# Two value products over 512 columns at once, with their weights in units of two row groups

## The chip, the cores and the metric

One core of a Trainium2 chip. The metric is the time of one launch on the device in microseconds; lower is better. The engines of the core are named as the profile names them: PE (matrix products), PEld (its weight loads), DVE and ACT (vector and scalar work), POOL, and SP, which issues the transfers.

## The reference, cut to what matters

One encoder layer over 512 tokens of width 1024, in float32. Three token mixers run side by side, their results are gated and summed, and a layer of 16 experts follows.

```python
z = jnp.einsum('bsd,df->bsf', x, w_in[l])
q_na, k_na, v_na, q_g, k_g, v_g, q_m, gate_logits = jnp.split(z, _split_points(), axis=-1)
y_na  = neighbourhood_attention(q_na, k_na, v_na, rpb)      # 8 heads of 64
y_gqa = gqa_attention(q_g, k_g, v_g, ...)                   # 8 query heads of 64, 2 key/value heads
mkv = jnp.einsum('bmd,df->bmf', mem, w_mem_kv[l])           # 256 memory tokens
mk, mv = jnp.split(mkv, 2, axis=-1)
y_mem = memory_attention(q_m, mk, mv)                       # 4 heads of 128
merged = jnp.sum(gates * proj, axis=2)
x = layer_norm(DN_ALPHA * x + merged @ w_out)
x = layer_norm(DN_ALPHA * x + expert_choice_ffn(x))
```

The change concerns two of these products: `mv`, 256 memory tokens by 1024 by 512 columns, and `v_na`, 512 tokens by 1024 by 512 columns.

## The kernel before

**Products in three parts.** Float32 operands are split into a high part (a copy to the type float32r, on ACT) and a low part (the source less the high part, on DVE); `hi_lo` (L91) issues both. A product is three matmuls for each of the 8 groups of 128 rows of the contraction: high by high, high by low, low by high, all added up in one bank of PSUM.

**Weights as a stream.** The weights of the mixers lie in memory as 74 units of 128 x 1024 (512 KB), in the order of use. `Stream` (L137) takes them through three steps: `_dma` issues the load of a unit into a raw buffer (SP), `_split` makes its high and low part (ACT, DVE), `take` hands it to a product. `prefetch(n)` splits ahead until n units beyond those taken are split, and then issues loads until two units (`AHEAD_DMA`) beyond the split ones are on their way. A load needs a raw buffer: units 2 to 9 have one each, all others share two (`raw_twin`), so a load waits for the subtraction of the unit two before it. A split needs a home: there are three for high parts (two buffers `whi`, one in `los`) and three for low parts (in `los`), taken in turn (`hi_tile`, `lo_tile`), so a split waits for the last product of the unit three before it.

A narrow unit (`nu` on the host) holds 256 columns of 512 rows: two of them make a product over 256 columns, which `n_chunk` (L290) issues for one block of 128 tokens: 8 x 3 = 24 matmuls, 256 columns each. A unit of the last product of the mixers (`wide`, units 66 to 73) holds 512 columns of 256 rows.

**The memory mixer.** `g_mem` (L317) makes four key products (`k_item`), the values (`v_item`, L347: two halves of 256 columns, two token blocks each, with the last two parts of the split of x among them), and four query products (`q_item`). Its units are 0 to 3, 4 to 7 and 8 to 11.

**The order of the work around the second product.** The order of every engine's instructions is the order in which the program issues them; each engine works through its own list. `run` (L782) drives a generator of products and, at each of its yields, takes a step of the attention pipeline (`Attn.step`, L754) at a given rate. One step issues, for three units of attention in flight: the scores of the newest (S) on PE, the transposes of the one before (T), the value product of the one before that (PV); then the softmax of the newest (row maxima on DVE, two exponentials on ACT), the evacuation of the transposes (half on DVE, half on ACT), the normalisation (DVE) and the split of the result. The scores have two banks of PSUM, the transposes two, the plain products three.

`g_na_v` (L461) is the value product of the neighbourhood mixer, units 30 to 33: two halves of 256 columns, for each half four token blocks, with a yield after each block, which makes eight yields. The last steps of the grouped attention fall on the first of them. After it two transfers copy the values shifted by half a tile (`v_shift`, L474), the transfers of the position bias follow, and then the mixer's query and key products (nqk, units 34 and 35).

```python
    run(g_branch(2, True), 1.0, 3)
    run(g_na_v(), 1.0)
    at.drain()
    na_bias(0)
    run(g_na_qk(0))
```

The experts' weights come through a ring of buffers (`Ring`), loaded as buffers become free.

Of the kernel before, what the change touches and what calls it, by code (L numbers as in the profile page):

```python
# [10 lines left out]
F32R = mybir.dt.float32r  # L11
# [7 lines left out]
P = 128  # L19
D = 1024  # L20
S = 512
KD = 8
NT = 4
# [41 lines left out]
def layer_kernel(ctx: ExitStack, tc: tile.TileContext, xt, xn, first0, wu, bgate, rpb, gains, wrt,  # L65
# [14 lines left out]
    def R(tag, shape, name, dt=F32, bufs=None):  # L80
        return rp.tile(shape, dt, name=name, tag=tag, bufs=bufs)
# [46 lines left out]

    los = R("Q9", [P, 4, 1024], "los", F32R)

    def hi_tile(i):
        if i % 3 == 2:
            return los[:, 3]
        return R("hi", [P, 1024], f"whi{i}", F32R, bufs=2)


    class Stream:  # L137
# [23 lines left out]
        def _split(self):  # L161
            i = self.ns
            if i >= self.nd:
                self._dma()
            raw = self.raw.pop(i)
            if i == N_UNITS - 1:
                both = R("VS", [P, 2, 1024], "wlast", F32R)
                hi, lo = both[:, 0], both[:, 1]
            else:
                hi = hi_tile(i)  # L170
                lo = lo_tile(i)
            hi_lo(hi, lo, raw)
            self.hl[i] = (hi, lo)
            self.ns += 1
# [7 lines left out]
        def take(self, n=1):  # L182
# [2 lines left out]
            r = [self.hl.pop(self.used + j) for j in range(n)]  # L185
            self.used += n
            return r

    def lo_tile(i):
        return los[:, i % 3]  # L190

    after = {}
    ws = Stream()
# [96 lines left out]
    def n_chunk(acc, us, ah, al, m, hooks={}):  # L290
        c = slice(m * P, (m + 1) * P)
        for k in range(KD):
# [4 lines left out]
            nc.tensor.matmul(acc, ah[:, k, c], lo, start=False, stop=False)  # L297
            nc.tensor.matmul(acc, al[:, k, c], h, start=False, stop=(k == KD - 1))

    def spin(n):  # L300
        for _ in range(n):
            nc.tensor.matmul(warm[:, :P], ident, ident, start=True, stop=True)
# [14 lines left out]
    def g_mem():  # L317
        zz = R("Q3", [P, 4, 1024], "mkvzs")
        ST["A5"] = zz[:, 0:2]
        ST["A6"] = zz[:, 2:4]  # L320
        mk = ST["A5"][:, 0].rearrange("p (h t) -> p h t", h=4)
        mv = ST["A6"][:, 0].rearrange("p (m f) -> p m f", m=2)
        qm = R("Q2", [P, 4, S], "qmT")
        ST.update(mkT=mk, mv=mv, qmT=qm)

        def k_item(h):
            u, = ws.take()
            ws.prefetch()
            acc = PB("mm", f"mk{h}")
            if h == 0:  # L330
                first_unit(acc[:, :256])
            else:
                t_unit(acc[:, :256], u, memh, meml, h == 1)
            if h >= 2:
                split_x(h - 2)
            yield
            nc.vector.tensor_copy(mk[:, h], acc[:, :256])

        def q_item(h):
            u, = ws.take()  # L340
            ws.prefetch()
            acc = PB("mm", f"qm{h}")
            t_unit(acc, u, xh, xl)
            yield
            nc.scalar.activation(qm[:, h], acc, AF.Copy, scale=1.0 / math.sqrt(128.0))

        def v_item(q):  # L347
            us = ws.take(2)
            for m in range(2):
                acc = PB("mm", f"mv{q}{m}")  # L350
                n_chunk(acc[:, :256], us, memh, meml, m)
                ws.prefetch(1 + m)
                if q == 0:
                    split_x(2 + m)
                yield
                nc.scalar.copy(mv[:, m, q * 256:(q + 1) * 256], acc[:, :256])

        for h in range(4):
            yield from k_item(h)
        for q in range(2):  # L360
            yield from v_item(q)
        for h in range(4):
            yield from q_item(h)

# [96 lines left out]
    def g_na_v():  # L461
        v = ST["b01"][:, 0:2].rearrange("p a (b f) -> p (a b) f", f=S)
        ST["v_na"] = v
        for q in range(2):
            us = ws.take(2)
            for m in range(NT):
                acc = PB("mm", f"nv{q}{m}")
                n_chunk(acc[:, :256], us, xh, xl, m)
                ws.prefetch(2 if m == NT - 1 else 1)
                yield  # L470
                nc.scalar.copy(v[:, m, q * 256:(q + 1) * 256], acc[:, :256])
        vs = R("VS", [P, 3, S], "v_shift")
        ST["v_shift"] = vs
        nc.sync.dma_start(vs[0:64], v[64:128, 0:3])  # L474
        nc.sync.dma_start(vs[64:128], v[0:64, 1:4])
# [1210 lines left out]
def _prep(inp):  # L1686
    import numpy as np
    f = np.float32
    x = np.asarray(inp["x"])[0]
    xp = _perm(x)  # L1690
    w_in = np.asarray(inp["w_in"])[0]
    w_mem = np.asarray(inp["w_mem_kv"])[0]
    w_br = np.asarray(inp["w_branch"])[0]
    w_out = np.asarray(inp["w_out"])[0]

    def tu(w, c):
        return w[:, c:c + 128].reshape(8, 128, 128).swapaxes(0, 1).reshape(128, 1024)

    def nu(w, c, h):
        return w[h * 512:(h + 1) * 512, c:c + 256].reshape(4, 128, 256).swapaxes(0, 1).reshape(128, 1024)  # L1700

    def wide(w, c, kp):
        return w[kp * 256:(kp + 1) * 256, c:c + 512].reshape(2, 128, 512).swapaxes(0, 1).reshape(128, 1024)

    def pu(g, jp):
        return w_br[g][:, jp * 256:(jp + 1) * 256].reshape(4, 128, 256).swapaxes(0, 1).reshape(128, 1024)

    gate = lambda g, j: tu(w_in, 2816 + g * 1024 + j * 128)
    mk = lambda h: [tu(w_mem, h * 128)]
    mv = lambda q: [nu(w_mem, 512 + q * 256, h) for h in range(2)]  # L1710
    qm = lambda h: [tu(w_in, 2304 + h * 128)]
    units = mk(0) + mk(1) + mk(2) + mk(3) + mv(0) + mv(1) + qm(0) + qm(1) + qm(2) + qm(3)
    units += [nu(w_in, 1536 + q * 256, h) for q in (2, 0, 1) for h in range(2)]
    for jp in range(4):
        units += [gate(2, 2 * jp), gate(2, 2 * jp + 1), pu(2, jp)]
    units += [nu(w_in, 1024 + q * 256, h) for q in range(2) for h in range(2)]
    qk = lambda hp: [tu(w_in, hp * 128), tu(w_in, 512 + hp * 128)]
    units += qk(0)
    for jp in range(4):
        units += [gate(1, 2 * jp), gate(1, 2 * jp + 1), pu(1, jp)]  # L1720
        if jp < 3:
            units += qk(jp + 1)
    units += [gate(0, j) for j in range(8)]
    units += [pu(0, jp) for jp in range(4)]
    units += [wide(w_out, o * 512, kp) for o in range(2) for kp in range(4)]
    assert len(units) == N_UNITS

    t = np.arange(512)
    b, r, c = t // 64, (t // 8) % 8, t % 8
    orig = r * 64 + b * 8 + c  # L1730
    inv = (f(10000.0) ** (-np.arange(0, 32, 2, dtype=f) / f(32))).astype(f)
    ang = np.concatenate([r.astype(f)[:, None] * inv, (b * 8 + c).astype(f)[:, None] * inv], -1).astype(f)
    csn = np.stack([np.cos(ang), np.sin(ang)], 1).astype(f)
    csn = csn.reshape(4, 128, 2, 32).swapaxes(0, 1)
    p = np.arange(128)
    s = 8 * (p // 64) + p % 8
    nmask = np.zeros((128, 3, 32), f)
    for ty in range(3):
        v = -8 * ty + np.arange(32)[None, :]
        lo = s - 8  # L1740
        lo = np.maximum(lo, 0) if ty == 0 else (np.minimum(lo, 0) if ty == 2 else lo)
        ok = (v >= lo[:, None]) & (v < lo[:, None] + 16)
        nmask[:, ty] = np.where(ok, 0.0, NEG)
    before = (orig[:, None] <= orig[None, :]).astype(np.float16)
    tri = np.stack([before[:128, 128:256], before[128:256, :128], before[:128, :128]])
    rpbp = np.zeros((8, 15, 63), f)
    rpbp[:, :, 16:47] = np.asarray(inp["na_rpb"])[0]
    rpbr = np.stack([rpbp[:, 7 - rr:15 - rr] for rr in range(8)])
    memt = np.asarray(inp["mem"])[0].T.reshape(8, 128, 256).swapaxes(0, 1)
    return {  # L1750
        "xt": xp.T.reshape(8, 128, 512).swapaxes(0, 1),
        "xn": xp.reshape(4, 128, 1024).swapaxes(0, 1),
        "first0": np.concatenate([memt.reshape(128, 4, 512), units[0].reshape(128, 4, 256)], -1),
        "wu": np.stack(units),
        "bgate": np.asarray(inp["b_gate"])[0].reshape(24, 128).T,
        "rpb": rpbr,
        "gains": np.stack([np.asarray(inp["gqa_q_gain"])[0], np.asarray(inp["gqa_k_gain"])[0]]),
        "wrt": np.asarray(inp["w_router"])[0].reshape(8, 128, 16).swapaxes(0, 1),
        "lnp": _norm_rows(*(np.asarray(inp[n])[0] for n in ("ln1_g", "ln1_b", "ln2_g", "ln2_b"))),
        "lnt": np.stack([np.asarray(inp[n])[0].reshape(8, 128).T for n in ("ln1_g", "ln1_b")], 1),  # L1760
        "wx": _expert_rows(np.asarray(inp["w_gate_up"])[0], np.asarray(inp["w_down"])[0]),
        "csn": csn, "nmask": nmask, "tri": tri,
        "iota": np.broadcast_to(np.arange(1, 65, dtype=f), (128, 64)),
    }
# [23 lines left out]
```

## Time and profile before

| | |
|---|---|
| median of 3 runs | 968.36 us (968.03 to 968.84) |
| the profiled execution | 967.9 us |
| its span, first to last instruction | 966.1 us, granted clock 0.998 |
| PE busy | 943.5 us, 98% of the span |
| value product of the memory (mv) | 96 matmuls of 256 columns, 19.7 to 31.2 us |
| value product of the last mixer (nv) | 192 matmuls of 256 columns, 212.0 to 247.4 us, five attention steps among them |

In the tables of the profile a row names line, engine, operation, output and inputs. In rows of the timeline the first number is the start and the second the duration, both in us, and in brackets stands how long the engine was idle before it and what ended that. "gs", "gt" and "gy" are scores, transposes and value product of the grouped attention, "pr" a branch product, "whi" and "los" the homes of split units.

### The profile page before, as it was taken

The page shows a single profiled execution, that of the slowest core. Times are in us where ns is not written, and L with a number is a line of the kernel's source. Part 1 is how long each engine was busy: PE and PEld are TensorE (multiplying, and loading weights), DVE is VectorE, ACT ScalarE, POOL GpSimd, SP SyncE. Part 2 cuts the span into 40 slices and gives each one's busy share as a digit, 9 for nine tenths or more (in the row PEclk, how much of TensorE's full clock was granted, in tenths as well). Part 3 has the DMA queues.
Part 4 walks back from the last instruction along what each step waited for, and adds up shares of the span by engine and source line. Part 5 has one row for each costly group of instructions (what it writes and reads, how often), then busy time and mean ns, then how long its engine had stood idle before and what let it go on. Part 6 is the DMA issues. An engine that isn't in the chain of part 4 may idle for free.

```text
span 966.1 us, 13195 instructions
## 1 busy us (share of the span) xinstructions
PE 943.5 (98%) x5406; PEld 615.1 (64%) x5406; DVE 453.0 (47%) x851; ACT 277.2 (29%) x545; POOL 84.6 (9%) x98
## 2 busy tenths in 40 slices
PE   9999999999999999999999999999999999998996
PEld 9899878889888888887885333433343333532344
DVE  6347668874376566237464212653322222231426
ACT  5334454544354454323242111100010001100123
POOL 0102303000022231000023000000000000000003
PEclk9999999999999999999999999999999999999999
DMA  9321111211333322575919999999999999999992
GB/s 361 113 67 66 66 66 44 67 61 50 102 104 105 100 82 84 213 285 206 370 50 373 410 427 433 430 428 431 432 428 430 431 431 429 431 430 432 428 408 94
DMA packets 38329, 251.19 MB, mean 260 GB/s; under 512 B 12911, under 2 KB 13295, under 8 KB 24830
## 3 DMA queue, kind: packets, MB, share of 16 engines
q1 hardware_dynamic: 37550, 249.74, 63.9%
q8 instruction: 42, 0.69, 0.3%
q10 hardware_dynamic: 720, 0.62, 0.2%
q14 instruction: 17, 0.14, 0.0%
HBM read 247.46 MB, written 2.10 MB: 258 GB/s over the span
## 4 chain that ended last, share of the span: by engine, by line
PE 80%; DMA 10%; DVE 6%; ACT 1%; issue 1%; POOL 1%; DVEq 0%; POOLq 0%; ACTq 0%; SPq 0%
DMA w<-in_wx 10%; PE g L1295 10%; PE u L1295 9%; PE y L1330 8%; PE gate L274 4%; PE gate L275 4%; PE gate L276 4%; PE pr L274 2%; PE gy L649 2%; PE ga L1255 2%; PE pr L275 2%; PE pr L276 2%; PE nqk L274 2%; PE nqk L276 2%; PE nqk L275 2%; PE gt L636 1%
## 5 line engine op out<-in xcount | busy, mean ns | idle before, releaser
L1295 PE MATMUL g<-w,xs 128*64 128x512 f32 x512 | 135.1, 606 | 4.0 <-DMA w<-in_wx 3.9
L1295 PE MATMUL u<-w,xs 128*64 128x512 f32 x512 | 131.6, 592 | 0.0
L1330 PE MATMUL y<-w,hT 128*64 128x512 f32 x480 | 106.6, 594 | 3.4 <-DMA w<-in_wx 2.7
L93 DVE TENSOR_TENSOR y<-y,y 64x512 fp32r<-64x512 f32 x30 | 20.7, 689 | 134.5 <-ACT y L92 134.5
L1295 PEld LDWEIGHTS u<-w,xs 128*64 128x64 f32 x512 | 36.8, 137 | 73.1 <-issue 72.3
L92 ACT CAST y<-y 64x512 fp32r<-64x512 f32 x30 | 17.4, 580 | 224.9 <-PE y L1330 213.6
L1330 PEld LDWEIGHTS y<-w,hT 128*64 128x64 f32 x480 | 33.8, 137 | 72.1 <-issue 63.8
L93 DVE TENSOR_TENSOR los<-raw_twin,whi 128x1024 fp32r<-128x1024 f32 x43 | 54.1, 1259 | 52.5 <-ACT whi L92 52.2
L276 PE MATMUL gate<-xh,los 128*128 128x512 f32 x192 | 74.8, 390 | 0.0
L1295 PEld LDWEIGHTS g<-w,xs 128*64 128x64 f32 x512 | 30.5, 136 | 55.4 <-issue 43.9
L274 PE MATMUL gate<-xh,whi 128*128 128x512 f32 x160 | 63.5, 397 | 0.0
L275 PE MATMUL gate<-xl,whi 128*128 128x512 f32 x160 | 62.3, 390 | 0.0
L1402 DVE TENSOR_TENSOR acc<-acc,cb 128x512 f32<-128x512 f32 x56 | 35.6, 683 | 37.8 <-PE cb L1400 37.8
L92 ACT CAST whi<-raw_twin 128x1024 fp32r<-128x1024 f32 x43 | 45.1, 1049 | 8.3 <-PE wo L1093 4.4
L1471 POOL TENSOR_TENSOR acc<-acc,ln2g 128x512 f32<-128x512 f32 x6 | 7.6, 1280 | 431.4 <-DVE l2s L1499 429.4
L93 DVE TENSOR_TENSOR los<-raw_twin,los 128x1024 fp32r<-128x1024 f32 x21 | 26.5, 1263 | 35.2 <-ACT los L92 35.1
L276 PEld LDWEIGHTS gate<-xh,los 128*128 128x128 f32 x192 | 36.0, 188 | 7.8
L625 ACT ACTIVATE att_twin<-gs,nm 128x512 f32<-128x512 f32 x32 | 21.7, 684 | 51.1 <-DVE nm L624 51.1
L1305 ACT ACTIVATE tg<-g 128x512 f32<-128x512 f32 x16 | 9.5, 597 | 90.5 <-PE g L1295 90.5
L274 PEld LDWEIGHTS gate<-xh,whi 128*128 128x128 f32 x160 | 30.0, 188 | 7.1 <-issue 1.2
L275 PEld LDWEIGHTS gate<-xl,whi 128*128 128x128 f32 x160 | 30.1, 188 | 5.9
L1318 DVE COPY hT<-ht 128x512 f32<-128x512 f32 x15 | 10.3, 690 | 44.4 <-PE ht L1313 44.4
(432 smaller groups left out, 1893.8 us busy)
## 6 DMA issues: line engine op xcount, KB each, us to landing
w<-in_wx SPq DMA_DIRECT2D x89, 2048.0 KB
raw_twin<-in_wu SPq DMA_DIRECT2D x65, 512.0 KB
w<-in_wx SPq DMA_DIRECT2D x14, 1024.0 KB
raw<-in_wu SPq DMA_DIRECT2D x8, 512.0 KB
xr<-in_xt SPq DMA_DIRECT2D x4, 512.0 KB
macc<-in_xn SPq DMA_DIRECT2D x2, 1024.0 KB
first<-in_first SPq DMA_DIRECT2D x4, 384.0 KB
bf<-in_rpb SPq DMA_DIRECT2D x64, 24.0 KB
```

The source lines that it names most:

```text
L92: nc.scalar.copy(hi, src)
L93: nc.vector.tensor_tensor(lo, src, hi.bitcast(F32), op=ALU.subtract)
L274: nc.tensor.matmul(acc, w_h, rh[:, k], start=(k == 0), stop=False)
L275: nc.tensor.matmul(acc, w_h, rl[:, k], start=False, stop=False)
L276: nc.tensor.matmul(acc, w_l, rh[:, k], start=False, stop=(k == nk - 1))
L625: nc.scalar.activation(self.p[:, h], self.s[h], AF.Exp, bias=nm[:, h:h + 1], accum_out=self.sm[:, h:h + 1])
L649: nc.tensor.matmul(self.y[h * 64:h * 64 + 64, :P], ST["vg"][:, kc, kvh * 64:kvh * 64 + 64], self.pt[:, h, kc], start=(kc == 0), stop=(kc = ...
L1255: nc.tensor.matmul(g, XH[:, m, c], oh[:, m, sl], start=(m == 0), stop=False)
L1295: nc.tensor.matmul(GU[e][b][hf * 64:hf * 64 + 64], xs, w[b][:, hf * 512:hf * 512 + 512], start=(k == 0), stop=(k == KD - 1))
L1318: nc.vector.tensor_copy(t, tp)
L1330: nc.tensor.matmul(y[o * 64:o * 64 + 64], hT[:, c, hf * 64:hf * 64 + 64], w[j][:, o * 512:(o + 1) * 512], start=(k == 0 and j == 0), stop= ...
L1402: nc.vector.tensor_tensor(a, a, cb, op=ALU.add)
```

## The change

The weights of mv and nv are laid out on the host as four `wide` units each: unit kp holds rows 256 kp to 256 kp + 255 of all 512 columns. A new `wide_part` issues the 2 x 3 matmuls of one such unit for one token block, each 512 columns wide. For mv the loop over units is outermost: two banks are open, each unit is taken, the next one prefetched, and the unit is multiplied with both token blocks; the two parts of the split of x stand in the first two turns, and the evacuations, now of 512 columns, at the end. For nv all four units are taken at once; each token block then goes through the four of them, with a prefetch after the second and a yield after the second and fourth, so that there are eight yields again. Since four units of nv are alive together, the third and fourth (units 32 and 33) get homes in a tile of their own on the buffers Q3 (`wide_v`), and the turn of the three homes goes on with unit 34 where unit 31 left it (`home`).

```diff
-    def hi_tile(i):
-        if i % 3 == 2:
-            return los[:, 3]
-        return R("hi", [P, 1024], f"whi{i}", F32R, bufs=2)
+    NV = 30
+    wide_v = []
+
+    def home(i):
+        if NV + 2 <= i < NV + 4:
+            if not wide_v:
+                wide_v.append(R("Q3", [P, 4, 1024], "whl_v", F32R))
+            j = 2 * (i - NV - 2)
+            return wide_v[0][:, j], wide_v[0][:, j + 1]
+        i = (i - 2 * (i >= NV + 4) - NV) % 3
+        return los[:, 3] if i == 2 else R("hi", [P, 1024], f"whi{i}", F32R, bufs=2), los[:, i]
...
+    def wide_part(acc, u, kp, ah, al, m):
+        c = slice(m * P, (m + 1) * P)
+        h, lo = (x.rearrange("p (k c) -> p k c", k=2) for x in u)
+        for k in range(2):
+            kk = 2 * kp + k
+            nc.tensor.matmul(acc, ah[:, kk, c], h[:, k], start=(kk == 0), stop=False)
+            nc.tensor.matmul(acc, ah[:, kk, c], lo[:, k], start=False, stop=False)
+            nc.tensor.matmul(acc, al[:, kk, c], h[:, k], start=False, stop=(kk == KD - 1))
...
-        def v_item(q):
-            us = ws.take(2)
+        def v_items():
+            accs = [PB("mm", f"mv{m}") for m in range(2)]
+            for kp in range(4):
+                u, = ws.take()
+                ws.prefetch()
+                for m in range(2):
+                    wide_part(accs[m], u, kp, memh, meml, m)
+                if kp < 2:
+                    split_x(2 + kp)
+                yield
             for m in range(2):
-                acc = PB("mm", f"mv{q}{m}")
-                n_chunk(acc[:, :256], us, memh, meml, m)
-                ws.prefetch(1 + m)
-                if q == 0:
-                    split_x(2 + m)
-                yield
-                nc.scalar.copy(mv[:, m, q * 256:(q + 1) * 256], acc[:, :256])
+                nc.scalar.copy(mv[:, m], accs[m])
...
     def g_na_v():
         v = ST["b01"][:, 0:2].rearrange("p a (b f) -> p (a b) f", f=S)
         ST["v_na"] = v
-        for q in range(2):
-            us = ws.take(2)
-            for m in range(NT):
-                acc = PB("mm", f"nv{q}{m}")
-                n_chunk(acc[:, :256], us, xh, xl, m)
-                ws.prefetch(2 if m == NT - 1 else 1)
-                yield
-                nc.scalar.copy(v[:, m, q * 256:(q + 1) * 256], acc[:, :256])
+        us = ws.take(4)
+        for m in range(NT):
+            acc = PB("mm", f"nv{m}")
+            for kp in range(4):
+                wide_part(acc, us[kp], kp, xh, xl, m)
+                if kp == 1:
+                    ws.prefetch(2 if m == NT - 1 else 1)
+                if kp % 2:
+                    yield
+            nc.scalar.copy(v[:, m], acc)
...
-    mv = lambda q: [nu(w_mem, 512 + q * 256, h) for h in range(2)]
-    units = mk(0) + mk(1) + mk(2) + mk(3) + mv(0) + mv(1) + qm(0) + qm(1) + qm(2) + qm(3)
+    units = mk(0) + mk(1) + mk(2) + mk(3) + [wide(w_mem, 512, kp) for kp in range(4)] + qm(0) + qm(1) + qm(2) + qm(3)
...
-    units += [nu(w_in, 1024 + q * 256, h) for q in range(2) for h in range(2)]
+    units += [wide(w_in, 1024, kp) for kp in range(4)]
```

More of the change, by code (lines that the diff above doesn't have):

```diff
@@ L169, in _split @@
             else:
-                hi = hi_tile(i)
-                lo = lo_tile(i)
+                hi, lo = home(i)
             hi_lo(hi, lo, raw)
@@ L187, in take @@
             return r
-    def lo_tile(i):
-        return los[:, i % 3]
     after = {}
@@ L345, in q_item @@
             nc.scalar.activation(qm[:, h], acc, AF.Copy, scale=1.0 / math.sqrt(128.0))
-        def v_item(q):
-            us = ws.take(2)
-            for m in range(2):
-                acc = PB("mm", f"mv{q}{m}")
-                n_chunk(acc[:, :256], us, memh, meml, m)
-                ws.prefetch(1 + m)
-                if q == 0:
-                    split_x(2 + m)
-                yield
-                nc.scalar.copy(mv[:, m, q * 256:(q + 1) * 256], acc[:, :256])
+        def v_items():
[8 more added lines that the diff above has]
+                yield
+            for m in range(2):
+                nc.scalar.copy(mv[:, m], accs[m])
         for h in range(4):
             yield from k_item(h)
-        for q in range(2):
-            yield from v_item(q)
+        yield from v_items()
         for h in range(4):
@@ L463, in g_na_v @@
         ST["v_na"] = v
-        for q in range(2):
-            us = ws.take(2)
-            for m in range(NT):
-                acc = PB("mm", f"nv{q}{m}")
-                n_chunk(acc[:, :256], us, xh, xl, m)
-                ws.prefetch(2 if m == NT - 1 else 1)
-                yield
-                nc.scalar.copy(v[:, m, q * 256:(q + 1) * 256], acc[:, :256])
+        us = ws.take(4)
[8 more added lines that the diff above has]
+            nc.scalar.copy(v[:, m], acc)
         vs = R("VS", [P, 3, S], "v_shift")
```

## The prediction

> **What bounds the kernel now.** I read the page first (busy shares, the chain that ended last), then the busy time by stretch, the waits, and at last the timeline around the two product stages.
>
> ```profile
> span 966.1 us, 13195 instructions
> PE 943.5 (98%) x5406; PEld 615.1 (64%) x5406; DVE 453.0 (47%) x851; ACT 277.2 (29%) x545; POOL 84.6 (9%) x98
> PE 80%; DMA 10%; DVE 6%; ACT 1%; issue 1%; POOL 1%; DVEq 0%; POOLq 0%; ACTq 0%; SPq 0%
> ```
>
> PE is busy nearly all the time and carries 80% of the chain. The two stages that the change touches, as stretches of time (engine columns: busy us and instructions; then granted clock, DMA share, GB/s):
>
> ```profile
> 19.60:31.10 11.50, 11.50 (x98) 11.50 (x97) 7.34 (x8) 7.11 (x9) 2.56 (x3) 1.00 0.67 247
> 212.00:247.30 35.30, 35.30 (x318) 32.97 (x317) 16.03 (x33) 14.09 (x34) 0.00 (x0) 1.00 0.14 46
> 262.00:440.00 178.00, 178.00 (x934) 148.30 (x933) 101.42 (x162) 75.71 (x148) 32.43 (x37) 1.00 0.42 144
> ```
>
> The first row is the memory's value product (mv), the second that of the last mixer (nv) with the end of the grouped attention in it, the third the rest of the mixers. PE has no gap in any of them, so a microsecond of PE work saved or lost here moves all that follows it, unless something that does not move with PE is late. The waits say whether there is such a thing:
>
> ```profile
> PE rT L406 <- POOL ropevg L400: 1.8, 1, 1.8
> SPq L817 <- PE u L1295: 222.9, 54, 10.5
> SPq L817 <- PE y L1330: 79.1, 24, 6.0
> ```
>
> The one long wait of PE in the mixers is for the rotary step on POOL, and the chain of waits leads from there back to PE:
>
> ```profile
> 105.94 0.91 PE my L596 x8
> ...
> 118.33 3.93 POOL ropevg L400 x2
> 122.30 0.66 PE rT L406 x4
> ```
>
> That POOL work follows PE's own work at 105.94, so it moves along. In the expert stage SP's loads wait mostly for PE's products to free their buffers (222.9 and 79.1 us), so that stage starts earlier or later with PE too. I carry every term below to the end at full size.
>
> **Narrow against wide products.** The change makes 48 matmuls of 512 columns from 96 of 256 in mv, and 96 from 192 in nv: 144 pairs become one matmul each, with the same multiply work. What a pair is worth is seen where mv (256 columns) meets the memory's query product (qm, 512 columns), which ends where gq begins:
>
> ```profile
> 19.71 0.28 PE L296 MATMUL mv<-whi,firsth 128*128 128x256 f32 x1
> 31.23 0.40 PE L274 MATMUL qm<-xh,los 128*128 128x512 f32 x1
> 53.02 0.28 PE L296 MATMUL gq<-whi,xh 128*128 128x256 f32 x1
> ```
>
> 96 starts of mv lie between 19.71 and 31.23: 11.52 us, 0.1200 each (the 0.28 is a modelled duration and overlaps the next; the distance of starts is what counts). The 96 of qm lie between 31.23 and 53.02: 21.79 us, 0.2270 each. Two narrow ones are 0.2400, so a pair saves 13 ns. mv: 11.52 − 48 × 0.2270 = **0.62 us**.
>
> The Trainium skill (TensorE: Matmul & The Clock Gate, Back-to-back issue gap) gives N/2.4 + 2.5 ns at full clock, which is 109 ns and 216 ns and would save only 2.6 ns a pair, an estimate of 0.37 us for all 144; the rows lie 11 ns above it at both widths, so the saving goes by the rows.
>
> In nv most products stand between pieces of attention, and the first matmul after such a piece starts slowly. There the like is the branch product pr (12 wide ones between a PV piece and the next scores) beside an nv block (24 narrow ones in the same place):
>
> ```profile
> 206.16 0.50 PE L274 MATMUL pr<-ym,los 128*128 128x512 f32 x1
> 209.05 0.39 PE L615 MATMUL gs<-kk,qs 128*128 128x512 f32 x1
> 211.95 0.39 PE L296 MATMUL nv<-whi,xh 128*128 128x256 f32 x1
> 214.93 0.40 PE L615 MATMUL gs<-kk,qs 128*128 128x512 f32 x1
> 217.85 0.38 PE L296 MATMUL nv<-whi,xh 128*128 128x256 f32 x1
> ```
>
> 2.89 us against 2.98: 0.09 saved. The new loop yields after every 12 wide matmuls, so there are eight blocks as before, with the same attention steps between them; six follow a PV piece (6 × 0.09 = 0.54), two follow a product (2 × (24 × 0.1200 − 12 × 0.2270) = 0.31). nv: **0.85 us**. Both together: 1.47 us, 0.15%.
>
> **What mv's new order asks of the splits.** With row groups outermost, each of its four units (4 to 7) is consumed in 12 × 0.227 = 2.7 us and none is needed again. What a split costs, from the groups of instructions (total us, mean ns):
>
> ```profile
> L92 ACT CAST xh<-xr 128x1024 fp32r<-128x1024 f32 x4 | 4.2, 1050 | 1.6 <-DMA xr<-in_xt 1.5
> L93 DVE TENSOR_TENSOR xl<-xr,xh 128x1024 fp32r<-128x1024 f32 x4 | 4.9, 1222 | 0.9 <-ACT xh L92 0.9
> ```
>
> Per unit ACT copies 1.05 us and DVE subtracts 1.22, and in the first two steps a part of x is split too: 2.1 us of ACT and 2.4 of DVE in 2.7 us, and units are split two ahead. It fits; the raw units there are eight buffers loaded far ahead. Cost nothing; if it did not fit, at most the 0.62 us would be lost. The two evacuations at the end are off the path: the memory attention reads them 20 us later.
>
> **What nv's new order asks.** Now all four units (30 to 33) are needed before the first token block is complete, so both late splits are put ahead of the first product; their results live in a tile of their own (Q3, whose last reader, the rotary step, is done long before). Then after the second row group of block 0 the next prefetch splits unit 34. That split is the trouble. In the order before, a unit is split only when its load has been in flight for a whole step; here the load of 34 may start only when the split of 32 has freed one of two raw buffers, and the split of 34 stands next in ACT's and DVE's queues, **ahead of the softmax** of the attention step that follows. Queued behind it on DVE: the row maxima, the evacuation of the transposes, the normalisation; on ACT: the two exponentials. For those waits PE: the scores of the following step need the score banks free, its transposes need the normalised rows.
>
> The split of unit 32 stands in the old order at the same place, so its times can be read off, and so can the load that it frees (the last line is GB/s in slices of 0.15 us from 214.0):
>
> ```profile
> 212.45 1.07 ACT L92 CAST los<-raw_twin 128x1024 fp32r<-128x1024 f32 x1
> 213.76 1.22 DVE L93 TENSOR_TENSOR los<-raw_twin,los 128x1024 fp32r<-128x1024 f32 x1
> 215.01 0.33 SPq L155 DMA_DIRECT2D raw_twin<-in_wu  x1
> GB/s 0 0 0 0 0 0 0 0 0 0 0 0 0 246 191 82 27 328 437 410 437 410 410 300 137 55 27 0 0 0 0 0 0 0 0 0 0 0 0 0
> ```
>
> Issued at 215.01, the load of 34 ends in the 27th slice, at 218.05. So ACT, done with unit 33 at about 214.6, stands still until 218.1. From ACT's copy to DVE's subtraction where DVE is free:
>
> ```profile
> 246.16 1.05 ACT L92 CAST los<-raw_twin 128x1024 fp32r<-128x1024 f32 x1 [1.07 <-PE nv L298]
> 247.24 1.23 DVE L93 TENSOR_TENSOR los<-raw_twin,los 128x1024 fp32r<-128x1024 f32 x1 [7.87 <-ACT los L92]
> ```
>
> 1.08 and 1.22 us: the row maxima start at 218.1 + 2.3 = 220.4 in place of 215.6. From there the softmax goes as it goes now:
>
> ```profile
> 215.60 1.29 DVE L624 TENSOR_REDUCE nm<-gs 128x1 f32<-128x512 f32 x2 [0.62 <-PE gs L616]
> 216.38 0.69 ACT L625 ACTIVATE att_twin<-gs,nm 128x512 f32<-128x512 f32 x1 [2.86 <-DVE nm L624]
> 217.06 0.68 ACT L625 ACTIVATE att_twin<-gs,nm 128x512 f32<-128x512 f32 x1
> 218.06 0.88 DVE L558 TENSOR_SCALAR att_twin<-att_twin,rc 128x512 f32<-128x512 f32 x2
> ```
>
> Exponentials at +0.78 and +1.46, normalised at +3.34: 221.2, 221.9 and 223.7. PE arrives at the next scores at 211.95 + 2.89 + 2.92 (attention piece, 214.93 to 217.85) + 2.89 = 220.65. What it would do there undisturbed:
>
> ```profile
> 220.81 0.40 PE L615 MATMUL gs<-kk,qs 128*128 128x512 f32 x1
> ...
> 221.74 0.27 PE L636 MATMUL gt<-ident,att_twin 128*128 128x128 f32 x1
> ...
> 222.71 0.33 PE L649 MATMUL gy<-att_twin,ropevg 128*64 128x128 f32 x2
> ```
>
> Scores to transposes 0.93, to PV 0.97 further: PV at 222.55. Instead the second head's transposes start at 223.7 and take half of 0.97: PV at 224.2. **Stall 1.67 us**, once: a step offers 5.8 us of PE, the chain of a step takes 3.3, so by the next scores it has caught up. The two splits at the front are not late: unit 32 is subtracted at 215.0 and 33 at 216.2, needed at 217.8 and 219.1. At the last block the split of unit 35 now comes after that block's first row group, 5 us before nv ends, where it came at the end before; nothing gets later by it, and the loads queued behind it on SP (the next raw unit, the shifted values, the bias rows) leave a little earlier, under PE work.
>
> **Sum.** −0.62 − 0.85 + 1.67 = +0.20 us. The profiled execution has 967.9 us beside its span of 966.1, which makes 968.1; the median of the runs is 968.36, 0.46 above that execution, so I say 968.6. A measurement of this kernel can tell about 0.2%, 1.94 us; the forecast lies within it. Bounds: the stall is nothing at least (then 968.36 − 1.47 = 966.9). At most the load of 35, issued 1.2 us after that of 34, halves its rate throughout: the transfer's 1.5 us (slices 17 to 26) doubled, stall 3.17, sum +1.70, 970.1. Near ends differ by 0.4 us with the spread of the runs (968.03 to 968.84).
>
> **Rivals.**
> *No stall* (0.18): the softmax has more slack than I reckon, or the load lands sooner, and only the products count: 966.9. For it: the same load of 0.5 MB has stood off the path all along. Against: the changed program's order has the split ahead of the row maxima on DVE and of the exponentials on ACT, and the old slack, from the end of the normalisation (218.94) to the second head's transposes (222.2), is some 3.3 us against a delay of 4.8. The Trainium skill (TensorE: Matmul & The Clock Gate, Architectural detail) says that ACT and DVE are strict first-in first-out; no row here tests that.
> *Loads together* (0.14), slower: if the load of 34 leaves only with the second split (1.2 us later, at 216.2) together with that of 35, and the two share the engines, it lands up to 2.7 us later; each microsecond goes into the stall, +2.9, 971.3. It passes 0.2% once the load lands after 219.8. Against: SP has the loads in the old order, and each waited for its own buffer so far (215.01 is right after the subtraction at 213.76 + 1.22).
> *No gain from width* (0.05): the wide products take twice the narrow ones, as they would were columns alone the price: sum +1.67, 970.0. The rows 0.1200 and 0.2270 speak against it.
>
> **Numbers.** The forecast has 0.58; 0.05 is left for what I do not see. Faster by over 0.2% needs no stall and 0.5 us from elsewhere: 0.05 of the first rival, 0.02 of the forecast and 0.03 of the rest, 0.10. Slower: 0.12 of the loads together, 0.01 of no gain, 0.02 each of forecast and rest, 0.17. Within: 0.73. The range runs from no stall less the spread of the runs, 966.5, to the shared load plus a little, 970.3.
>
> **What would show it.** In the profile after: mv from its first matmul to qm's first in 10.9 us at 0.227 a start; nv blocks of 2.89 us; ACT idle some 3.5 us in front of the first copy after the two of Q3, put down to the load of raw_twin; PE idle about 1.7 us at scores and transposes of the second attention step in nv, and nowhere else anew; all stages behind shifted by one constant of a few tenths. I am wrong if PE shows no such gap, if it shows one at several steps, or if the expert stage's length changes by over a microsecond.

## The result, and the profile after

The changed kernel takes 969.59 us (median of 14 runs, 968.78 to 971.62) against 968.06 us (967.5 to 969.08): a ratio of 1.0016, 95% interval 1.0009 to 1.0023. It is 1.5 us slower: the interval leaves out "no change", the ratio lies within 0.2% as forecast, and the time is a microsecond above the 968.6 of the forecast and inside its range.

The page after (the profiled execution took 970.67 us, a microsecond over its median):

```profile
span 968.9 us, 12898 instructions
PE 943.8 (97%) x5262; PEld 607.9 (63%) x5262; DVE 453.2 (47%) x851; ACT 276.5 (29%) x539; POOL 84.7 (9%) x98
PE 75%; DMA 14%; DVE 6%; ACT 2%; issue 2%; POOL 1%; DVEq 0%; POOLq 0%; ACTq 0%; SPq 0%
```

PE has the 144 matmuls less. The waits of PE in the mixers name one new row:

```profile
PE rT L419 <- POOL ropevg L413: 1.8, 1, 1.8
PE gs L630 <- ACT att_twin L640: 1.5, 1, 1.5
```

The timeline of PE at the two stages (first matmul of mv, of qm, of nv, of nqk):

```profile
20.54 0.40 PE L308 MATMUL mv<-whi,firsth 128*128 128x512 f32 x1
31.45 0.39 PE L277 MATMUL qm<-xh,los 128*128 128x512 f32 x1
212.12 0.50 PE L308 MATMUL nv<-whi,xh 128*128 128x512 f32 x1
248.98 0.39 PE L277 MATMUL nqk<-xh,los 128*128 128x512 f32 x1
```

mv takes 10.91 us (11.52 before), nv 36.86 (35.45 before). And the place of the wait, on ACT, DVE and PE:

```profile
212.62 2.02 ACT L92 CAST whl_v<-raw_twin 128x1024 fp32r<-128x1024 f32 x2
218.67 1.05 ACT L92 CAST los<-raw_twin 128x1024 fp32r<-128x1024 f32 x1 [4.03 <-DMA raw_twin<-in_wu]
221.67 0.69 ACT L640 ACTIVATE att_twin<-gs,nm 128x512 f32<-128x512 f32 x1 [1.95 <-DVE nm L639]
219.75 1.22 DVE L93 TENSOR_TENSOR los<-raw_twin,los 128x1024 fp32r<-128x1024 f32 x1 [3.47 <-ACT los L92]
220.90 1.28 DVE L639 TENSOR_REDUCE nm<-gs 128x1 f32<-128x512 f32 x2
222.50 0.50 PE L630 MATMUL gs<-kk,qs 128*128 128x512 f32 x1 [1.53 <-ACT att_twin L640]
222.84 0.39 PE L631 MATMUL gs<-kk,qs 128*128 128x512 f32 x1
223.17 0.50 PE L630 MATMUL gs<-kk,qs 128*128 128x512 f32 x1
223.51 0.40 PE L631 MATMUL gs<-kk,qs 128*128 128x512 f32 x1
223.98 1.06 PE L651 MATMUL gt<-ident,att_twin 128*128 128x128 f32 x8
```

ACT splits units 32 and 33 at once and then stands 4.03 us until the load of 34 lands; DVE stands behind it; the row maxima start at 220.9; PE stands 1.53 us at the next scores, because the exponentials have not freed the score banks. This is the chain that the prediction drew as far as the row maxima, which come 0.3 us later than it said (8.78 us after nv's first matmul in place of 8.45). Its last link is another: the sum let the second head's transposes wait for the normalised rows, and here PE waits at the scores and no more at the transposes. By the stages it comes to −0.61 + 1.41 = +0.80 us, and 1.5 were measured (0.9 to 2.2 by the interval). The experiments had to say whether the wait is the whole cause, and where the other 0.7 is.

Further on this execution has an expert stage (first gather to the end of the span) of 450.1 us against 449.0; in the ten runs below it is 448.5 to 450.1 with no order to it, and a second profile of the changed kernel has 449.0, so that is scatter. The same holds for the start: mv begins at 19.2 to 20.5 us in the twelve profiles, at 20.54 in this one and at 19.22 in the second of the same kernel.

### The profile page after: what moved, and what is told of

Read it like the earlier page. It is cut to its first block, busy times and chain, and to the rows that moved or that the text cites. A ratio compares the mean times of both kernels' runs of the same rounds, so it can differ in the third digit from the quotient of the medians.

```text
span 968.9 us, 12898 instructions
## 1 busy us (share of the span) xinstructions
PE 943.8 (97%) x5262; PEld 607.9 (63%) x5262; DVE 453.2 (47%) x851; ACT 276.5 (29%) x539; POOL 84.7 (9%) x98
## 4 chain that ended last, share of the span: by engine, by line
PE 75%; DMA 14%; DVE 6%; ACT 2%; issue 2%; POOL 1%; DVEq 0%; POOLq 0%; ACTq 0%; SPq 0%
DMA w<-in_wx 13%; PE g L1310 8%; PE u L1310 8%; PE y L1345 8%; PE gate L277 4%; PE gate L279 4%; PE gate L278 4%; PE ga L1270 2%; PE pr L277 2%; PE nqk L279 2%; PE nqk L277 2%; PE nqk L278 1%; PE gy L664 1%; PE ga L1272 1%; PE pr L278 1%
## 5 line engine op out<-in xcount | busy, mean ns | idle before, releaser
L277 PE MATMUL gate<-xh,whi 128*128 128x512 f32 x144 | 57.2, 397 | 0.0
L278 PE MATMUL gate<-xl,whi 128*128 128x512 f32 x144 | 56.1, 390 | 0.0
L277 PEld LDWEIGHTS gate<-xh,whi 128*128 128x128 f32 x144 | 27.0, 188 | 6.5 <-issue 1.2
L278 PEld LDWEIGHTS gate<-xl,whi 128*128 128x128 f32 x144 | 27.1, 188 | 5.3
```

The source lines that it names most:

```text
L277: nc.tensor.matmul(acc, w_h, rh[:, k], start=(k == 0), stop=False)
L278: nc.tensor.matmul(acc, w_h, rl[:, k], start=False, stop=False)
```

## The experiments

All times are against runs of the kernel before on the same chip: 968.17 us for the first four, 968.52 for the next three, 968.24 for the last three.

**1. The late split.** The prefetch that splits unit 34 moves to the second token block.

```diff
-                if kp == 1:
+                if kp == 1 and m:
                     ws.prefetch(2 if m == NT - 1 else 1)
```

> The changed kernel with one edit: the prefetch that splits unit 34 comes in the second token block of nv in place of the first, so the softmax of the next attention step no longer stands behind it. Theory A (the wait for the load of unit 34 in front of the softmax is the whole loss): no wait of PE at the scores in nv, nv 34.6 us from its first matmul to nqk's (35.45 before, 36.86 in the changed kernel), mv 10.9 us; the time 1.5 us below the kernel before, about 966.6. Theory B (the new order of homes and the tile on Q3 cost some 0.7 us in the stages behind, the expert stage above all): nv as in A, but the time only 0.8 below the kernel before, 967.3. Theory C (the stall has another cause, the width or the two open loads): the wait at the scores stays, time 1 to 1.5 us above the kernel before.

Measured: 966.70 us, −1.47, ratio 0.999 (0.9982 to 0.9999). PE has no wait in nv:

```profile
211.04 0.50 PE L308 MATMUL nv<-whi,xh 128*128 128x512 f32 x1
245.61 0.39 PE L277 MATMUL nqk<-xh,los 128*128 128x512 f32 x1
```

34.57 us, 0.88 below the kernel before: theory A. The time's interval (0.1 to 1.7 us below) has room for B's 0.8 too, but the homes and the tile on Q3 are the same here, and from nqk's first matmul to the output product's the profile has 199.25 us as before, so in the mixers they cost nothing. This kernel has the lowest median of all.

**2. Only mv wide.** nv, its units and the homes as before.

> Only mv is made wide; nv, its units and the homes are as before. Theory A: mv 10.9 us in place of 11.5, everything else the same length, time 0.6 us below the kernel before. Theory B: the same, since the homes are the old ones. If a microsecond saved in front of the expert stage is not carried to the end, the time is that of the kernel before.

Measured: 967.81 us, −0.36, ratio 0.9996 (0.9987 to 1.0004). In the profile mv takes 10.91 us:

```profile
20.00 0.40 PE L305 MATMUL mv<-whi,firsth 128*128 128x512 f32 x1
30.91 0.39 PE L274 MATMUL qm<-xh,los 128*128 128x512 f32 x1
```

The 0.61 us are there; in the time they cannot be told from nothing by this interval, nor from 0.6.

**3. Only nv wide.** mv as before.

> Only nv is made wide, with the homes and the order of splits of the changed kernel; mv is narrow. Theory A: PE waits 1.5 us at the scores and some more at the transposes, nv 36.9 us, time 1.4 us above the kernel before. Theory B: nv the same, time 2.1 us above. With the run of mv alone the two should add up to the changed kernel (+1.5 us measured).

Measured: 970.45 us, +2.28, ratio 1.0022 (1.0012 to 1.0031); nv 36.84 us, wait 1.6. With experiment 2 that adds up to +1.9. The stage is as A says; the median lies nearer to B, but the interval (1.2 to 3.0 us) holds A's 1.4 as well. If there is a surplus, nv's stage in this profile does not show it.

**4. The new order without the width.** Narrow products, but all four units of nv taken at once, with the homes of the changed kernel, and unit 34 split after the first block.

```diff
+        us4 = ws.take(4)
         for q in range(2):
-            us = ws.take(2)
+            us = us4[2 * q:2 * q + 2]
             for m in range(NT):
                 acc = PB("mm", f"nv{q}{m}")
                 n_chunk(acc[:, :256], us, xh, xl, m)
-                ws.prefetch(2 if m == NT - 1 else 1)
+                if q == 0 and m == 0:
+                    ws.prefetch(1)
+                elif q == 1 and m == NT - 1:
+                    ws.prefetch(2)
```

> No wide product at all (mv and nv narrow, units as before), but nv takes its four units at once, with the homes of the changed kernel, and splits unit 34 after the first narrow block: the order of splits without the width. Theory A: the wait at the scores appears with narrow products too, a little shorter since each block is 0.09 us longer: nv 35.45 + 2.1 = 37.5 us, time 2.1 us above the kernel before. Theory B: 2.8 above. Theory C (the width is the cause): nv 35.4 us and the time of the kernel before.

Measured: 971.49 us, +3.32, ratio 1.0031 (1.002 to 1.0043). The wait is there without any wide product (1.4 us at the scores), so C falls. But nv took 39.2 us, 1.7 more than the wait explains. The busy time by stretch shows why (the third number from the end is the granted clock of PE):

```profile
220.00:224.00 4.00, 2.56 (x14) 1.55 (x12) 3.59 (x7) 2.24 (x7) 0.00 (x0) 1.00 0.41 143
224.00:228.00 4.00, 3.93 (x27) 3.29 (x28) 3.55 (x9) 2.52 (x8) 0.00 (x0) 0.57 0.02 5
```

One of the four microseconds alone:

```profile
225.00:226.00 1.00, 1.00 (x9) 0.67 (x9) 1.00 (x3) 0.78 (x3) 0.00 (x0) 0.50 0.05 16
```

Behind the wait PE's clock falls to half: 0.57 on the mean of 4 us is half speed for 3.44 us. This became theory D: a wait costs more than its length, because in part of the executions the clock falls behind it.

**5. The early load.** The order of the splits stays, but unit 34's raw data go to a buffer of their own.

```diff
             if 2 <= i < 10:
                 ...
+            elif i == NV + 4:
+                t = ST["b01"][:, 3]
             else:
                 t = twin("raw")
```

> The changed kernel, its order of splits untouched, but the raw data of unit 34 go to a buffer of their own (a part of the rotary step's that is free by then), so that the load leaves right behind that of unit 33 and has landed long before its split. Theory A (the load in front of the softmax is the loss, not the splits themselves): ACT copies unit 34 right after 32 and 33, the row maxima start about 217.5 instead of 220.9, no wait of PE, nv 34.6 us, the time 1.5 us below the kernel before (966.7, like the late split). Rival (three splits in a row in front of the softmax are too much by themselves): PE still waits some tenths to 1 us at the scores or transposes, time 0.5 to 1 us below the kernel before.

Measured: 967.47 us, −1.05, ratio 0.9988 (0.9979 to 0.9997), no wait of PE, nv 34.57 us. ACT and DVE now go from the second split to the third without a gap:

```profile
213.51 1.06 ACT L92 CAST los<-ropevg 128x1024 fp32r<-128x1024 f32 x1
215.19 1.22 DVE L93 TENSOR_TENSOR los<-ropevg,los 128x1024 fp32r<-128x1024 f32 x1
216.32 1.28 DVE L641 TENSOR_REDUCE nm<-gs 128x1 f32<-128x512 f32 x2
```

Three splits ahead of the softmax fit; it was the load in front of it that did not. The time's interval (0.3 to 2.0 us below) holds the rival's price as well as A's; it is the missing wait and nv's length that decide. Experiments 1 and 5 take the wait away by different means and give the same nv.

**6 and 7. The wait filled with work.** Six extra wide matmuls ahead of the scores at which PE waits, into a bank that nothing reads; in the changed kernel (shown) and, ahead of the same scores, in the narrow one of experiment 4.

```diff
+                if m == 0 and kp == 3:
+                    pad = PB("mm", "pad")
+                    for _ in range(6):
+                        nc.tensor.matmul(pad, xh[:, 0, :P], xh[:, 1], start=True, stop=True)
```

> The changed kernel with six extra matmuls of 512 columns into a bank that nothing reads, put ahead of the scores at which PE waits (some 1.4 us of work into a wait of 1.5). Theory D (beside the wait itself of 1.4 us net in nv, PE's clock falls to half for some 3.4 us after the idle stretch in part of the executions, as the run of the narrow kernel in the new order showed it at 224 to 228): the fill keeps the clock up, the time falls from 1.5 or more above the kernel before to about 0.8 above (mv -0.62, nv +1.4), no execution over 970.5. Rival (no such cost; the surplus is scatter): the time stays at 1.5 above the kernel before, or rises by what the fill overlaps.

> The narrow kernel in the new order of splits (3.3 us above the kernel before) with the same fill ahead of the scores at which PE waits. Theory D: granted clock 1.00 from 224 to 228 us, nv about 37.4 us in place of 39.2, the time 2.0 to 2.2 above the kernel before. Rival (the surplus does not come from the clock): 3.3 above.

Measured: 968.97 us, +0.45, ratio 1.0003 (0.9994 to 1.0012), and 970.37 us, +1.85, ratio 1.0018 (1.0009 to 1.0028). The changed kernel without the fill is at +1.5, the narrow one at +3.3: more work on PE, and medians over a microsecond lower, though in both pairs the intervals overlap. One execution of experiment 6 is at 970.75, over the 970.5 that theory D allowed; it has the lowest clock of the eleven, 0.995. nv is no shorter by the fill itself (36.81 us against 36.86); in the narrow kernel it is 37.60 in place of 39.20, at full clock:

```profile
220.00:224.00 4.00, 3.90 (x20) 2.52 (x19) 3.58 (x9) 2.37 (x7) 0.00 (x0) 1.00 0.40 133
224.00:228.00 4.00, 4.00 (x42) 3.66 (x41) 2.93 (x7) 2.37 (x7) 0.00 (x0) 1.00 0.02 4
```

**8 to 10. A longer wait, bare and filled, and the changed kernel again.** In 8 the load of unit 34 takes the raw buffer that unit 33 frees, so it leaves later and with that of 35; 9 is the same with twelve extra matmuls; 10 is the changed kernel, unaltered.

```diff
             else:
+                if i == NV + 4:
+                    twins["raw"][1] += 1
                 t = twin("raw")
```

> The changed kernel, with the load of unit 34 put into the raw buffer that unit 33 frees (not 32), so that it leaves some 1.2 us later and together with that of unit 35. Both theories: ACT waits for the load until about 220 in place of 218.7, PE's wait at the scores grows from 1.5 to 2.8 us or more, and the time rises by as much. Theory D (the clock falls after a long enough idle stretch): in the profile the granted clock is 0.5 for some 3.4 us behind the wait, the slowed pieces cost a further 1 to 2 us, nv 39 to 40 us, and the time lies 4 to 4.5 above the kernel before. Rival (idle time alone): clock 1.00, nv 38.1 us, 2.8 above the kernel before.

> The same later load, with twelve extra wide matmuls (2.7 us) ahead of the scores at which PE waits. Theory D: clock 1.00, nv 38 us, the time 2 to 2.5 above the kernel before, well below the run without the fill. Rival: the same time as without the fill.

> The changed kernel once more, unchanged, on the chip of these runs, to set the filled and the unfilled wait side by side. Theory D: 1.2 to 1.6 us above the kernel before, with single executions 2.5 or more above; if the surplus over the 0.8 us that its stages show was scatter, about 0.8.

Measured: 8: 972.03 us, +3.79, ratio 1.0033 (1.0021 to 1.0046); 9: 970.43, +2.19, ratio 1.0021 (1.0012 to 1.003); 10: 969.76, +1.52, ratio 1.0014 (1.0005 to 1.0023). The wait in 8 is 2.7 us, nv 37.99, and its profile shows the clock at 1.00, against theory D:

```profile
220.00:224.00 4.00, 1.34 (x6) 0.52 (x4) 3.02 (x4) 2.05 (x6) 0.00 (x0) 1.00 0.30 114
224.00:228.00 4.00, 3.92 (x32) 2.95 (x32) 3.54 (x9) 2.64 (x9) 0.00 (x0) 1.00 0.07 27
```

But that execution took 970.52, and of the five the others lie at 970.88, 972.03, 972.21 and 972.28. The fill takes 1.6 us off the median, while nv in its profile is 37.90. The profile of 10 shows in the changed kernel itself what experiment 4 had shown:

```profile
220.00:224.00 4.00, 2.75 (x12) 1.79 (x12) 3.59 (x9) 2.29 (x7) 0.00 (x0) 0.88 0.33 131
224.00:228.00 4.00, 4.00 (x26) 3.24 (x25) 2.24 (x6) 2.48 (x7) 0.00 (x0) 0.69 0.00 0
```

0.88 and 0.69 on the mean are 1.0 and 2.5 us at half speed, 3.44 together; nv goes from 210.84 to 249.12:

```profile
210.84 0.50 PE L308 MATMUL nv<-whi,xh 128*128 128x512 f32 x1
249.12 0.39 PE L277 MATMUL nqk<-xh,los 128*128 128x512 f32 x1
```

38.28 us against 36.86 in the first profile of the same kernel, 1.42 more. So the same 1.5 us of waiting costs either itself or itself and 1.4 us more.

**What the clocks of all executions say.** The profile is of one execution, but the mean granted clock of every execution is on record. In all twelve profiles the clock is at half speed in the last 4.2 to 7.3 us, which lowers the mean to between 0.996 and 0.998; a fall of 3.44 us takes off another 0.0018. So, if the end is like that of the profiles, an execution at 0.997 or 0.998 has no such fall, one at 0.994 or 0.995 has one somewhere, and 0.996 can be either.

| | executions | at 0.995 or less | median at 0.997 and 0.998, above the like of the kernel before |
|---|---|---|---|
| 4, narrow, bare wait | 7 | 2 | +2.1 (2 executions) |
| 7, narrow, filled | 11 | 0 | +2.4 (6) |
| 8, longer wait, bare | 5 | 1 | +2.7 (2) |
| 9, longer wait, filled | 11 | 1 | +2.3 (8) |
| 10, changed kernel, bare | 11 | 0 | +1.7 (10) |
| 6, changed kernel, filled | 11 | 1 | +0.65 (10) |

In the narrow kernel and with the longer wait, the executions without a fall lie 1.1 to 1.3 us nearer to the kernel before than the medians of all (+3.3 and +3.8), and the gap to the filled kernels is all but gone, as theory D has it; these are two executions each. In the changed kernel itself it is otherwise: ten of the eleven executions of experiment 10 and twelve of the fourteen of the first comparison have no fall, and these too lie 1.7 and 1.4 us above. The two longest times of the first comparison, 970.94 and 971.62, are the two at 0.995; the median is not made by them. So the clock does not explain what the changed kernel's median has over the +0.80 of its stages, nor what the fill took off there.

## Why the prediction was right, and where it was off

*Width.* 0.62 forecast for mv, 0.61 measured; 0.85 for nv, 0.88 where nothing waits (experiments 1 and 5). The neighbours' distances of starts, 0.1200 and 0.2270, were the right prices, and the rival that width gains nothing is out.

*The wait.* Its place, its cause and its number (once) were right, and experiments 1, 4 and 5 show the cause: it comes without the width and goes when the split or the load is moved. Its size was 1.67 us; 36.86 − 34.57 = 2.29 were measured. Two links were too short. The load landed some 0.4 us later than 218.05 (counted from nv's start): the load of 35 followed it after 1.1 us and the two shared the engines, as the GB/s (slices of 0.15 us from 214.0) show against the 410 to 437 of before; SP's row covers both issues:

```profile
215.18 1.46 SPq L162 DMA_DIRECT2D raw_twin<-in_wu  x2
...
GB/s 0 0 109 0 0 0 0 0 0 0 0 0 0 0 109 246 191 191 382 246 300 328 410 437 328 328 300 382 300 273 300 300 273 273 273 191 191 109 191 109
```

I had put this in the upper bound and not in the sum. And PE starts slowly behind the wait: from the first scores to the transposes it takes 1.48 us (222.50 to 223.98) where I took 0.93, since the scores stand 0.34 apart in place of 0.23. They do so with the wait filled too (1.49 us in experiment 6), and why was not tried. The sum reached its last term by another way, the normalised rows; at those no wait is seen, the binding wait is the one at the score banks.

*No stall* is refuted, *loads together* true in part: they shared the engines, but the load of 34 was not held up until the second split. Experiment 8 is that rival made real, +3.8 us where I had written +2.9 (+2.7 in its two executions without a fall of the clock). One figure beside the sum was off: the formula quoted there saves its 2.5 ns a pair, not 2.6, and 0.36 us in all; nothing rests on it.

*What I had not seen.* By its stages the forecast sum of +0.20 becomes +0.80; the times say +1.5. That the result still lies within 0.2% is in part luck: the limit was 1.94 us, the interval reaches 2.2, and the forecast had no term for the rest. A step that the prediction lacked is that PE's clock may fall behind a wait. Shown: the fall in two of the five profiles with a bare wait (experiments 4 and 10) and in none of three with a filled one; by the clocks on record, 8 of 46 executions with a bare wait have 0.995 or less, against 2 of 33 with a filled one and 5 of 107 of kernels without this wait (the kernel before beside experiments 1 to 10, and experiments 1, 2 and 5). It accounts for the long times in experiments 4 and 8, but not for the median of the changed kernel. That the fill works through the clock is not shown there, and the cause of the 0.7 us stays open; a part of it may be scatter, since 0.80 lies just below the interval of the first comparison and inside that of experiment 10 (0.5 to 2.2 us). The Trainium skill (TensorE: Matmul & The Clock Gate, What's actually happening) describes this gate: half the pulses after an idle window of about 3.4 us, in windows that run freely. The length agrees (3.44 us at half speed, twice); the condition does not: here a wait of 1.4 to 1.5 us was enough in some executions, and 2.7 us was not in one. What decides in which executions it falls stays open.

## What to carry to other kernels

Before a split or copy is moved ahead in an engine's queue, look up when its load can leave and land, and which short, urgent work stands behind it: here one copy with 4 us to wait for cost 2.3 us in its stage, and 144 saved matmuls gave 1.5. Price a matmul by the distance of starts in the same company (behind attention, behind a product), not by its bar. And a wait on PE of a microsecond or two may cost more than it lasts, by a fall of the clock that one profile need not show. Read the granted clock of every execution before you put a surplus down to it: here it explained the longest times of two experiments, and not the median of the kernel that it was called in for.

## What the runs showed of the hardware that was not expected

PE's granted clock fell to half for 3.44 us after a wait of only 1.4 to 1.5 us in some executions of the same program, and cost 1.4 us there (nv 38.28 against 36.86). The fall came with a delay: in experiment 4 the wait ended at 222.59 and the clock fell only between 224 and 225 (0.78 on that microsecond's mean, 0.50 on the next). Six matmuls into an unread bank, put into the wait, did not lengthen nv (36.81 against 36.86); that they make the kernel faster is not shown beyond the noise (+0.45 against +1.5, with intervals that overlap). Two loads of 512 KB that leave 1.1 us apart moved about 300 GB/s together, less than one alone (410 to 437).
